# Output projection in scaled 16-bit halves, its weights resident from attention on, and the next layer's first weights made beside it

## Chip, cores, metric

One core of a Trainium2 chip runs the whole program. The metric is device time in microseconds (us), the median of several executions. The profile and the trace are of one execution.

## What is computed

Two layers of a token mixer, over 256 context tokens and 2048 latent tokens of width 1024. Each layer ends in one output projection and a gated residual. Cut from the reference:

```
for l in range(DEPTH):                      # DEPTH = 2, D = 1024
    shift, scale, gate = split(silu(c) @ w_mod[l] + b_mod[l], 3)
    h = rmsnorm(x, norm_g[l]) * (1 + scale) + shift
    f, g, (q, k, v, a) = branches(h @ w_in[l])        # Fourier, gated MLP, attention
    o = attention(q, k, v) * silu(a)                  # 8 heads, 2304 keys
    x = x + gate * (concat[f, g, o] @ w_out[l])       # w_out: 1024 x 1024
# the context rows y go the same way, in layer 0 alone
```

## The kernel before

A token tile is 128 rows; there are 18 (2 of context, 16 latent). A layer has three stages. The *blocks* normalise tiles and multiply them by five groups of input weights (group 0: keys, 416 columns; group 1: queries; groups 2 to 4: gates). *Attention* goes over heads and blocks of 512 queries. For each pair of key tiles TensorE makes the scores (`sc`), ScalarE takes two exponentials of each (a 16-bit `pp` and a 32-bit `pw`), GpSimd (one time in four VectorE) takes their difference, and TensorE multiplies both by the values (`pv`). VectorE reduces the row maxima (`mx`) of scores to come. Beside this runs a generator `background()`, advanced two steps a pair: the Fourier branch, then the gate vector (`modulate_turned(l, y, (2,), ..)`), and in layer 0 the small weights of layer 1 (`prepare`). The *output projection* follows: `mixed(t)` loads a tile of the concatenation, transposes it on TensorE and splits it into a high and a low part; `outward(l, y, t, n, ..)` makes half n of the output columns by `project`, 24 matmuls of 128x512 (8 chunks, three products: high x high, high x low, low x high), multiplies by the gate row `gr`, adds the residual and stores. In layer 0 `modulate_turned(l + 1, nxt, (0, 1), ..)` makes layer 1's shift and scale beside it: 32 loads into `mw`, two VectorE products with sums each.

All token products but the output projection use two 16-bit halves of each operand. The output projection uses two float32r parts: `weights` splits `w_out` (tags `wh`, `wl`, eleven buffers in pool W and five in pool X), and `mixed` takes one `h9` buffer a tile. Pool X opens only when attention's pool B has closed, so nothing that lives in it starts earlier.

Every operation is recorded first. A planner (`Plan.schedule`) with its own costs then gives each engine one fixed order, which may bring an operation forward past up to 1000 recorded ones where its buffers and operands allow it. All loads and stores are issued by SyncE, also in a fixed order. Since one helper emits everything, all instructions carry one line number (448).

Of the kernel before, what the change touches and what calls it, by code (L numbers as in the profile page):

```python
# [10 lines left out]
F32 = mybir.dt.float32  # L11
# [10 lines left out]
P = 128  # L22
D = 1024
# [38 lines left out]
XB = 6  # L62
# [487 lines left out]
def hybrid_kernel(ctx: ExitStack, tc: tile.TileContext, a: dict, out: bass.AP):  # L550
# [33 lines left out]
    def large():  # L584
        return mk(main, [P, T], F32R, "h9", 6)

# [3 lines left out]
    def k5():  # L590
        return mk(main, [P, NT * 65], F32, "k5")
# [325 lines left out]
    def operand():  # L917
        h = large()
        parts = h[:, :2 * D].rearrange("p (s k n) -> p s k n", s=2, k=KC)
        return parts[:, 0], parts[:, 1]  # L920

# [42 lines left out]

    def mixed(t):
# [12 lines left out]
        return hh, hl  # L978
# [26 lines left out]
    def weights(parts, wp, scale=None, extra=None):  # L1005
        n = sum(c for _, c in parts)
        wt = []
        for k in range(KC):
            wf = mk(wp, [P, NB], F32, "wf", WF)[:, :n]
            c0 = 0  # L1010
            for get, c in parts:
                get(k, wf[:, c0:c0 + c])
                c0 += c
            if extra and k >= WB - KC:
                wh, wl = (mk(extra, [P, NB], F32R, s, 2 * KC - WB) for s in ("wh", "wl"))
            else:
                wh, wl = (mk(wp, [P, NB], F32R, s, WB)[:, :n] for s in ("wh", "wl"))
            if scale is not None and k >= 4:
                v = scale[:, k - 4:k - 3]
                act.activation(out=wh, in_=wf, func=AF.Copy, scale=v)  # L1020
                dve.scalar_tensor_tensor(out=wl, in0=wf, scalar=v, in1=f(wh), op0=ALU.mult, op1=ALU.subtract)
            else:
                split(wh, wl, wf, pool if k % 2 else dve)
            wt.append((wh, wl))
        return wt

    def project(ht, wt, n):
        o = bank(tag="pj")
        hh, hl = ht
# [670 lines left out]
    for l in range(DEPTH):  # L1700
# [4 lines left out]
        def background():  # L1705
# [6 lines left out]
            load = lambda: mk(pools["W"], [P, NB], F32, "wh", WB)  # L1712
            for _ in modulate_turned(l, y, (2,), load):
# [8 lines left out]
        for b, blk in enumerate(blocks):  # L1722
# [7 lines left out]
            def done():  # L1730
# [3 lines left out]
        plan.close(pa)  # L1734
        pools["B"] = opened("B", "left")
        plan.close(wp)
# [4 lines left out]
        wp = pools["W"]  # L1741
        plan.close(pools["B"])
        px = opened("X", "left")
        tiles = list(range(0 if l < DEPTH - 1 else CT, NT))
        wt = [weights([(lambda k, dst, n=n: sp.dma_start(out=dst, in_=a["w_out"][l, k * P:(k + 1) * P, n * NB:(n + 1) * NB]), NB)], wp, y["vinv"], px if n else None)
              for n in range(2)]
        for t in tiles[:XB]:
            hts[t] = mixed(t)
        load = lambda: mk(px, [P, NB], F32, "mw", MW)
        ahead = iter(()) if l == DEPTH - 1 else modulate_turned(l + 1, nxt, (0, 1), load)  # L1750
        for t in tiles[:-XB]:
# [5 lines left out]
        for t in tiles[-XB:]:  # L1757
            outward(l, y, t, 0, hts[t], wt[0])
        for i, t in enumerate(tiles[-XB:]):
            outward(l, y, t, 1, hts[t], wt[1])  # L1760
            if l < DEPTH - 1 and i == 2:
                bounded(nxt)
# [3 lines left out]
        plan.close(px)  # L1766
        wt = {}
        plan.close(pools["C"])
        plan.close(wp)
        if l < DEPTH - 1:  # L1770
            pa_[0] = pa = opened("A", "left")
            wp = opened("W", "right")
            nxt["ic"] = [None] * 5
# [105 lines left out]
```

## Time and profile before

| | |
|---|---|
| median of 3 runs | 3146.82 us (3145.03 to 3150.45) |
| profiled execution, its own time | 3142.39 us |
| its span, first to last instruction | 3140.6 us |
| TensorE busy, granted clock (mean) | 2953.2 us (94%), 0.973 |
| VectorE, ScalarE, GpSimd busy | 2458.5, 1826.3, 1693.5 us |
| layer 0: blocks, attention, output projection | to about 650, 1430, 1677 us |
| layer 1: blocks, attention, output projection | to about 2200, 2932, 3140 us |

Busy TensorE time contains matmuls that overlap in the pipeline, so the time of a matmul in a stream is taken from start to start. A clock of 1.00 is 2.4 GHz; values below 1 are means over stretches at 2.4 and 1.2 GHz.

### The profile page before, as it was taken

What the parts mean: (1) busy time and instruction counts of PE and PEld (TensorE: products, weight loads), DVE (VectorE), ACT (ScalarE), POOL (GpSimd) and SP (SyncE); (2) the same over time, 40 slices, a digit from 0 to 9 for tenths busy, and PEclk for the clock granted to TensorE, in tenths of its full rate; (3) what the DMA queues carried; (4) which work ended last, traced back from release to release, by engine and by line L of the source; (5) the groups of instructions that cost most, each with busy time, mean ns of one, the idle gap of its engine ahead of it and who ended that gap; (6) DMA issues with size and microseconds to landing.
All of it is one profiled execution on the core that took longest, in us unless ns stands there. A gap on an engine that the chain in (4) does not pass through costs nothing.

```text
span 3140.6 us, 64404 instructions
## 1 busy us (share of the span) xinstructions
PE 2953.2 (94%) x23194; PEld 1724.2 (55%) x23194; DVE 2458.5 (78%) x6740; ACT 1826.3 (58%) x3904; POOL 1693.5 (54%) x1836
## 2 busy tenths in 40 slices
PE   6789999899999999998999999998999999999899
PEld 3445555445554555556785454553555555555687
DVE  7878788789999978765638888887899989887332
ACT  4553444167777788883006644531887887888400
POOL 3564444357667777772004744542876777777300
PEclk8899999999999999999999999998999999999999
DMA  7333344422324322205535343345023241230342
GB/s 271 69 73 58 84 94 87 102 88 67 86 61 131 81 72 61 57 23 177 175 118 192 62 86 86 87 96 142 24 64 79 71 125 49 61 75 20 111 134 81
DMA packets 487865, 289.08 MB, mean 92 GB/s; under 512 B 372316, under 2 KB 424180, under 8 KB 487544
## 3 DMA queue, kind: packets, MB, share of 16 engines
q1 hardware_dynamic: 487544, 284.96, 35.1%
q8 instruction: 182, 2.98, 0.4%
q14 instruction: 139, 1.14, 0.1%
HBM read 193.18 MB, written 91.66 MB: 91 GB/s over the span
## 4 chain that ended last, share of the span: by engine, by line
PE 59%; DVE 20%; DMA 8%; ACT 6%; POOL 3%; issue 2%; SPq 2%; DVEq 0%; ACTq 0%; POOLq 0%
PE pj L448 20%; PE sc L448 16%; PE pv L448 10%; PE mx L448 9%; DVE k L448 6%; DVE mx L448 4%; PE cb L448 3%; DMA k<-d 2%; ACT k L448 2%; SPq L448 2%; POOL k L448 2%; ACT pp L448 1%; DVE ns_t L448 1%; DMA mw<-in_w_modT_dram 1%; ACT pw L448 1%
## 5 line engine op out<-in xcount | busy, mean ns | idle before, releaser
L448 POOL TENSOR_TENSOR pp<-pw,pp 128x512 f16<-128x512 f32 (+1 forms) x876 | 1021.0, 1183 | 395.9 <-ACT pw L448 317.6
L448 PEld LDWEIGHTS <-h 128*128 128x128 f16 (+2 forms) x7008 | 581.8, 98 | 772.2 <-issue 410.2
L448 DVE TENSOR_REDUCE mx<-mx 128x1 f32<-128x512 f32 (+1 forms) x1296 | 770.9, 626 | 142.9 <-PE mx L448 136.9
L448 ACT ACTIVATE pp<-sc 128x512 f16<-128x512 f32 (+1 forms) x1168 | 717.5, 615 | 228.8 <-PE sc L448 215.5
L448 PE MATMUL sc<-h,h 128*128 128x512 f16 (+1 forms) x2336 | 602.8, 380 | 4.1 <-ACT pw L448 1.7
L448 ACT ACTIVATE pw<-sc 128x512 f32<-128x512 f32 (+1 forms) x876 | 543.7, 621 | 0.6 <-POOL pp L448 0.6
L448 PEld LDWEIGHTS <-pp 128*128 128x128 f16 x10432 | 467.3, 98 | 115.1 <-issue 32.5
L448 PE MATMUL pv<-k,pp 128*128 128x65 f16 (+2 forms) x10432 | 507.6, 203 | 7.6 <-DVE sm L448 7.0
L448 PE MATMUL mx<-h,h 96*128 96x512 f16 (+1 forms) x1296 | 410.4, 366 | 34.9 <-DVE mx L448 25.5
L448 PE MATMUL pj<-wh,h 128*128 128x512 f32 x1088 | 361.9, 405 | 7.3 <-DVE k L448 7.1
L448 PEld LDWEIGHTS <-hp 128*128 128x128 f16 x1920 | 187.8, 99 | 176.0 <-issue 14.3
L448 PE MATMUL pj<-w,h 128*128 128x512 f16 (+1 forms) x1296 | 272.2, 349 | 4.8 <-DVE tm L448 3.6
L448 PE MATMUL pj<-w,hp 128*128 128x512 f16 (+1 forms) x1152 | 241.4, 347 | 8.5 <-DVE tm L448 4.5
L448 POOL TENSOR_TENSOR h<-k,h 128x512 f16<-128x512 f32 (+1 forms) x72 | 80.8, 1138 | 299.6 <-ACT h L448 298.4
L448 PEld LDWEIGHTS pj<-wh,h 128*128 128x128 f32 x1088 | 208.6, 192 | 56.7 <-DVE k L448 11.1
L448 DVE TENSOR_TENSOR pp<-sc,pp 128x512 f16<-128x512 f32 (+1 forms) x292 | 197.8, 677 | 42.6 <-ACT sc L448 39.7
L448 PE MATMUL sc<-h 40*128 40x512 f16 (+1 forms) x1168 | 228.2, 387 | 0.0
L448 PE MATMUL pj<-wl,h 128*128 128x512 f32 x544 | 216.8, 399 | 0.0
L448 PE MATMUL pj<-h,h 128*128 128x416 f16 (+2 forms) x912 | 201.7, 363 | 6.5 <-ACT h L448 5.0
L448 DVE TENSOR_TENSOR pj<-pj,gr 128x512 f32<-128x512 f32 x68 | 47.3, 698 | 187.3 <-PE pj L448 187.3
L448 PE MATMUL pj<-h,hp 128*128 128x512 f16 (+1 forms) x768 | 174.4, 365 | 6.4 <-ACT hp L448 3.3
L448 ACT ACTIVATE sc<-sc 128x512 f32<-128x512 f32 (+1 forms) x292 | 178.8, 612 | 0.0
(270 smaller groups left out, 3936.7 us busy)
## 6 DMA issues: line engine op xcount, KB each, us to landing
d<-k SPq DMA_DIRECT2D x560, 48.0 KB
d<-k SPq DMA_DIRECT2D x166, 128.0 KB
d<-k SPq DMA_DIRECT2D x70, 256.0 KB
k<-d SPq DMA_DIRECT2D x132, 128.0 KB
k<-d SPq DMA_DIRECT2D x66, 256.0 KB
h<-d SPq DMA_DIRECT2D x24, 432.0 KB
d<-vt SPq DMA_DIRECT2D x144, 65.0 KB
k<-d SPq DMA_DIRECT2D x16, 585.0 KB
```

The costliest lines, as they stand in the source:

```text
L448: r = getattr(getattr(self.nc, eng), method)(*args, **kw)
```

## The change

`w_out` of the layer is loaded and split during attention by a new generator `output_weights`, into two float16 halves after scaling by a power of two (`power`, `halve` are the helpers that the other weights use). All 16 pieces stay in pool W (`wo`). `mixed` scales each row of its tile by a power of two from the row's sum of squares and splits into float16 halves, two tiles to a `h9` buffer; `outward` undoes both scalings in the gate multiplication. Tiles are prepared 4 ahead, not 6; `k5`, which holds a tile on its way in, has 3 buffers, not 2. In layer 0 `onward` makes shift and scale (into `mw` in pool W, 6 buffers of which 4 hold the condition vectors), then the weights of groups 0 and 2 of layer 1, in a new pool G. The order of the two halves changes: tile by tile to the end.

```diff
-TICKS = 2
+TICKS = 2, 1
+AHEAD_G = 2,
+OPACE = 3
-WB, WF = 11, 3
+WF = 3
-MW = 8
+MW = 6
-XB = 6
+XB = 4
     def k5():
-        return mk(main, [P, NT * 65], F32, "k5")
+        return mk(main, [P, NT * 65], F32, "k5", 3)
...
     def mixed(t):
         xt = k5()[:, :D]
...
-        hh, hl = operand()
+        ss = mk(small, [P, 1], F32, "ss")
+        act.activation(out=k2([P, D], BF16), in_=xt, func=AF.Square, accum_out=ss)
+        dve.tensor_scalar(out=ss, in0=ss, scalar1=2.0 ** -100, scalar2=2.0 ** 100, op0=ALU.max, op1=ALU.min)
+        pq = mk(small, [P, 2], F32, "mq", XB + 2)
...
+        dve.tensor_scalar(out=pq[:, 1:], in0=pq[:, 1:], scalar1=ow["pw"][:, 1:], scalar2=None, op0=ALU.mult)
+        act.activation(out=xt, in_=xt, func=AF.Copy, scale=pq[:, 0:1])
+        if t % 2 == 0:
+            mpair[0] = stacked()
...
         for half in range(2):
...
-            split(hh[:, 4 * half:4 * half + 4], hl[:, 4 * half:4 * half + 4], tp)
+            s = slice(4 * half, 4 * half + 4)
+            act.activation(out=hh[:, s], in_=tp, func=AF.Copy)
+            dve.tensor_tensor(out=hl[:, s], in0=tp, in1=hh[:, s], op=ALU.subtract)
...
+    def output_weights(l, y, wp):
+        w = mk(wp, [P, KC, 2, 2, NB], F16, "wo", 1)
+        am = mk(small, [P, 2 * KC + 1], F32, "wa", 1)
+        for k in range(KC):
+            for n in range(2):
+                sp.dma_start(out=whole(w[:, k, n]), in_=a["w_out"][l, k * P:(k + 1) * P, n * NB:(n + 1) * NB])
+                i = 2 * k + n
+                dve.tensor_reduce(out=am[:, i:i + 1], in_=whole(w[:, k, n]), axis=AX.X, op=ALU.max, apply_absolute_value=True)
+                yield
...
+        for k in range(KC):
+            for n in range(2):
+                halve(w[:, k, n], r[:, max(0, k - 3):max(0, k - 3) + 1], mk(wp, [P, NB], F32, "wf", WF))
+                yield
...
-        dve.tensor_tensor(out=o, in0=o, in1=y["gr"][1 if t < CT else 0][:, ns], op=ALU.mult)
+        dve.scalar_tensor_tensor(out=o, in0=o, scalar=ht[2], in1=y["gr"][1 if t < CT else 0][:, ns], op0=ALU.mult, op1=ALU.mult)
...
             gates(l, y, pools["C"])
+            for _ in output_weights(l, y, pools["W"]):
+                for _ in range(OPACE):
+                    yield
...
+        def onward():
+            for _ in modulate_turned(l + 1, nxt, (0, 1), lambda: mk(pools["W"], [P, NB], F32, "mw", MW)):
+                yield
+            bounded(nxt)
+            nxt["ic"] = [None] * 5
+            wt[0] = group(l + 1, nxt, 0, wp)
...
+            for g in AHEAD_G:
+                wt[g] = group(l + 1, nxt, g, wp)
...
+        for t in tiles:
             for n in range(2):
-                outward(l, y, t, n, hts[t], wt[n])
-                for _ in range(TICKS):
+                outward(l, y, t, n, hts[t], ow["w"][n])
+                for _ in range(TICKS[n]):
                     next(ahead, None)
-            hts[t + XB] = mixed(t + XB)
+            if t + XB < NT:
+                hts[t + XB] = mixed(t + XB)
```

VectorE at the end of layer 0's attention. The first piece is of before: its first products of `mw` for layer 1's shift stand behind the last attention work and among the splits of the projection (`h`, `wl`).

```order
L448 SCALAR_TENSOR_TENSOR wl_22749<-wf_19750,vinv_930,wh_22736 128x512
L448 SCALAR_TENSOR_TENSOR wl_22761<-wf_19817,vinv_930,wh_22742 128x512
L448 TENSOR_TENSOR h_4574_22708<-cx_22725,h_4574_22708 128x512
L448 TENSOR_TENSOR h_4588_22756<-cb_22744,h_4588_22756 128x512
L448 TENSOR_TENSOR h_4588_22756<-cx_22776,h_4588_22756 128x512
L448 SCALAR_TENSOR_TENSOR k_4594_22796,acc_22797<-mw_22734,mw_22715 128x512
L448 TENSOR_TENSOR pj_22657<-pj_22657,gr_3121_15553 128x512
L448 SCALAR_TENSOR_TENSOR k_4599_22812,acc_22797<-mw_22734,mw_22719 128x512
```

This piece is of the change, at the last two exponential differences (`pp`) of the same attention and the last `rc`, which ends it.

```order
L450 SCALAR_TENSOR_TENSOR k_4621_22749,acc_22397<-mw_22664,mw_19301 128x512
L450 SCALAR_TENSOR_TENSOR k_4626_22782,acc_22397<-mw_22664,mw_19317 128x512
L450 TENSOR_TENSOR pp_22784<-sc_22751,pp_22784 128x512
L450 SCALAR_TENSOR_TENSOR k_4633_22821,acc_22397<-mw_22723,mw_19298 128x512
L450 SCALAR_TENSOR_TENSOR k_4636_22828,acc_22397<-mw_22723,mw_19305 128x512
L450 SCALAR_TENSOR_TENSOR k_4639_22853,acc_22397<-mw_22819,mw_19301 128x512
L450 SCALAR_TENSOR_TENSOR k_4644_22894,acc_22397<-mw_22819,mw_19317 128x512
L450 TENSOR_TENSOR h_4596_22618<-cx_22861,h_4596_22618 128x512
L450 SCALAR_TENSOR_TENSOR k_4647_22910,acc_22397<-mw_22855,mw_19298 128x512
L450 SCALAR_TENSOR_TENSOR k_4650_22938,acc_22397<-mw_22855,mw_19305 128x512
L450 TENSOR_TENSOR h_4596_22618<-cx_22912,h_4596_22618 128x512
L450 RECIPROCAL rc_22958<-pv_22582 128x1
```

Of the 64 products, 48 now stand ahead of this last `rc` and 16 behind it; before, all 64 stood behind it.

TensorE at the border between layer 0 and layer 1. Before, the last product of layer 0 (`wh`) was followed by the two small transposes and products that find the scale of group 0 and group 1 (`am`, `pe`), and then by group 0's first matmul (`h,hp`, 416 columns).

```order
L448 MATMUL pj_24435<-wh_22830,h_4810_23991 128x512
L448 MATMUL cx_24523<-ident_163,k_4843_24319 128x128 x4
L448 MATMUL cb_24566<-ident_163,am_24321 1x128
L448 MATMUL cb_24594<-pe_24569,ones_157 128x2
L448 MATMUL cb_24605<-ident_163,am_24459 1x128
L448 MATMUL cb_24636<-pe_24613,ones_157 128x2
L448 LDWEIGHTS hp_24545
L448 MATMUL pj_24651<-h_4835_24272,hp_24545 128x416
```

In the change group 0's first matmul follows one normalisation transpose.

```order
L450 LDWEIGHTS h_4857_24352
L450 MATMUL pj_24778<-wo_13692,h_4857_24352 128x512
L450 MATMUL cx_24854<-ident_163,k_4876_24469 128x128 x4
L450 LDWEIGHTS h_4897_24657
L450 MATMUL pj_24860<-h_4756_23611,h_4897_24657 128x416
```

The scale of group 0 is found earlier, among the projection's tiles.

ScalarE near the end of layer 0's attention in the change: a Square and a scaling Copy of 128x1024, for tiles of the projection, stand among the exponentials. Two of each do so in either layer; before, none did.

```order
L450 ACTIVATE pw_21671<-sc_21618 128x512
L450 ACTIVATE pp_21682<-sc_21662 128x512
L450 ACTIVATE sc_21662<-sc_21662 128x512
L450 ACTIVATE sm_21773<-pv_21378 128x192
L450 ACTIVATE sm_21773<-pv_21378 128x64
L450 ACTIVATE k_3960_19557<-k_3960_19557,mq_21675 128x1024
L450 ACTIVATE pp_21796<-sc_21759 128x512
```

The Copy moved in front of the exponentials of the pair that follows.

## Rows read from the trace of the kernel before

**Rows 1.** Page, first part: busy us, share of the span, instructions.

```profile
PE 2953.2 (94%) x23194; PEld 1724.2 (55%) x23194; DVE 2458.5 (78%) x6740; ACT 1826.3 (58%) x3904; POOL 1693.5 (54%) x1836
```

**Rows 2.** Busy time by stretches of attention and output projection.

```profile
core 0: us, PE busy (x) PEld busy (x) DVE busy (x) ACT busy (x) POOL busy (x), PEclk, DMA share, GB/s
650.00:950.00 300.00, 292.89 (x3043) 167.59 (x3042) 282.78 (x622) 229.54 (x499) 205.36 (x191) 0.99 0.28 74
1250.00:1390.00 140.00, 135.34 (x1416) 74.53 (x1412) 111.28 (x241) 115.40 (x237) 103.55 (x100) 0.98 0.21 54
1390.00:1430.00 40.00, 39.13 (x483) 22.70 (x483) 10.93 (x24) 38.99 (x82) 35.50 (x34) 1.00 0.04 8
1430.00:1550.00 120.00, 102.26 (x481) 80.21 (x479) 79.63 (x208) 17.70 (x32) 3.52 (x4) 0.93 0.66 203
1550.00:1676.00 126.00, 126.00 (x580) 102.51 (x578) 52.38 (x114) 16.69 (x34) 4.83 (x8) 1.00 0.46 147
...
2890.00:2930.00 40.00, 39.13 (x470) 22.04 (x468) 12.65 (x26) 39.57 (x83) 34.47 (x33) 1.00 0.04 8
2930.00:2970.00 40.00, 32.83 (x210) 25.95 (x208) 15.66 (x25) 12.45 (x23) 5.31 (x6) 0.91 0.54 169
```

**Rows 3.** Chain that ended last, from 2900 us: start, duration, engine, what.

```profile
2934.15 5.35 DMA k<-d
...
3008.51 0.44 PE cx L448 x4
...
3081.67 52.65 PE pj L448 x228
```

**Rows 4.** TensorE in order of time, 1754 to 1761 us: start, us, operation, count.

```profile
1756.14 4.05 PE L448 MATMUL pj<-w,hp 128*128 128x512 f16 x18
1760.02 0.81 PE L448 MATMUL pj<-w,h 128*128 128x512 f16 x3
```

**Rows 5.** TensorE in order of time: the projections' ends, and layer 1's start.

```profile
1430.64 0.48 PE L448 MATMUL pj<-wh,h 128*128 128x512 f32 x1
...
1677.39 0.60 PE L448 MATMUL cx<-ident,k 128*128 128x128 f32 x4
...
1686.84 11.04 PE L448 MATMUL pj<-h,hp 128*128 128x416 f16 x48
...
1699.32 3.85 PE L448 MATMUL pj<-h,h 128*128 128x416 f16 x21 [0.27 <-ACT k L448]
1703.01 0.33 PE L448 MATMUL cx<-ident,ck 128*128 128x128 f32 x1
...
2932.45 0.48 PE L448 MATMUL pj<-wh,h 128*128 128x512 f32 x1
...
3135.31 0.39 PE L448 MATMUL pj<-wh,h 128*128 128x512 f32 x1
```

**Rows 6.** TensorE's waits, 1430 to 1690 us: total us, times, longest.

```profile
PE cx L448 <- DMA k<-d: 9.1, 6, 3.2
PE pj L448 <- DVE k L448: 7.1, 2, 3.7
```

**Rows 7.** Groups by shape: busy us, mean ns, idle before.

```profile
L448 DVE SCALAR_TENSOR_TENSOR k<-wh,wh 128x512 bf16<-128x512 f32 x64 | 58.6, 931 | 0.0
L448 DVE SCALAR_TENSOR_TENSOR k<-mw,mw 128x512 bf16<-128x512 f32 x64 | 40.9, 686 | 17.3 <-DMA mw<-in_w_modT_dram 14.4 <-DMA d<-k 1.5 <-DMA wf<-in_w_out_dram 1.3
L448 ACT ACTIVATE k<-k 128x1024 bf16<-128x1024 f32 x36 | 38.1, 1058 | 46.3 <-DMA k<-in_x_dram 17.2 <-DMA k<-d 15.8 <-DMA k<-in_ctx_dram 5.4
L448 POOL TENSOR_TENSOR w<-k,w 128x512 f16<-128x512 f32 x32 | 36.5, 1161 | 2.3 <-ACT w L448 2.3
L448 ACT ACTIVATE k<-w,wr 128x512 f32<-128x512 f32 x32 | 21.4, 712 | 2.1 <-DVE wr L448 1.5 <-POOL w L448 0.5
L448 DVE TENSOR_REDUCE am<-w 128x1 f32<-128x512 f32 x32 | 20.7, 671 | 0.4 <-DMA w<-in_w_g_dram 0.4
L448 ACT ACTIVATE w<-k 128x512 f16<-128x512 f32 x32 | 18.5, 618 | 0.0
```

More of the change, by code (lines that the diff above doesn't have):

```diff
@@ L914, in prepare @@
         yield
[L917 to L920, printed above, removed]
     hpair = [None]
@@ L963, in norm @@
         return hh, hl
+    mpair = [None]
     def mixed(t):
@@ L969, in mixed @@
         sp.dma_start(out=xt[:, 512:], in_=tokens(mo_d, t))
-        hh, hl = operand()
+        ss = mk(small, [P, 1], F32, "ss")
+        act.activation(out=k2([P, D], BF16), in_=xt, func=AF.Square, accum_out=ss)
+        dve.tensor_scalar(out=ss, in0=ss, scalar1=2.0 ** -100, scalar2=2.0 ** 100, op0=ALU.max, op1=ALU.min)
+        pq = mk(small, [P, 2], F32, "mq", XB + 2)
+        pi = pq.bitcast(I32)
+        dve.tensor_scalar(out=pi[:, 0:1], in0=ss.bitcast(I32), scalar1=-0.5, scalar2=1597463007.0 + float(TOP << 23),
+                          op0=ALU.mult, op1=ALU.add)
+        dve.tensor_scalar(out=pi[:, 0:1], in0=pi[:, 0:1], scalar1=EXPO, scalar2=None, op0=ALU.bitwise_and)
+        dve.tensor_scalar(out=pi[:, 1:], in0=pi[:, 0:1], scalar1=-1.0, scalar2=float(254 << 23), op0=ALU.mult, op1=ALU.add)
+        dve.tensor_scalar(out=pq[:, 1:], in0=pq[:, 1:], scalar1=ow["pw"][:, 1:], scalar2=None, op0=ALU.mult)
+        act.activation(out=xt, in_=xt, func=AF.Copy, scale=pq[:, 0:1])
+        if t % 2 == 0:
+            mpair[0] = stacked()
+        parts = mpair[0][:, t % 2, :2 * D].rearrange("p (s k n) -> p s k n", s=2, k=KC)
+        hh, hl = parts[:, 0], parts[:, 1]
         for half in range(2):
@@ L1003, in resident @@
         return [(v(k)[:, 0], v(k)[:, 1]) for k in range(KC)]
-    def weights(parts, wp, scale=None, extra=None):
-        n = sum(c for _, c in parts)
-        wt = []
+    ow = {}
+    def output_weights(l, y, wp):
+        w = mk(wp, [P, KC, 2, 2, NB], F16, "wo", 1)
+        am = mk(small, [P, 2 * KC + 1], F32, "wa", 1)
         for k in range(KC):
[L1009 to L1025, printed above, removed]
+            for n in range(2):
[3 more added lines that the diff above has]
+                yield
+        late = am[:, KC:2 * KC].rearrange("p (k n) -> p k n", n=2)
+        dve.tensor_tensor(out=late, in0=late, in1=y["vinv"].unsqueeze(2).to_broadcast([P, 4, 2]), op=ALU.mult)
+        dve.tensor_reduce(out=am[:, 2 * KC:], in_=am[:, :2 * KC], axis=AX.X, op=ALU.max)
+        pw = mk(lay, [P, 2], F32, "pwo")
+        power(am[:, 2 * KC:], pw)
+        r = mk(small, [P, 5], F32, "wq", 1)
+        dve.tensor_copy(r[:, 0:1], pw[:, 0:1])
+        dve.tensor_scalar(out=r[:, 1:], in0=y["vinv"], scalar1=pw[:, 0:1], scalar2=None, op0=ALU.mult)
+        yield
[3 more added lines that the diff above has]
+                yield
+        ow["pw"] = pw
+        ow["w"] = [[(w[:, k, n, 0], w[:, k, n, 1]) for k in range(KC)] for n in range(2)]
@@ L1027, in project @@
     def project(ht, wt, n):
         o = bank(tag="pj")
-        hh, hl = ht
+        hh, hl = ht[:2]
         for k in range(KC):
@@ L1711, in background @@
             pools["C"] = opened("C", "right")
-            load = lambda: mk(pools["W"], [P, NB], F32, "wh", WB)
-            for _ in modulate_turned(l, y, (2,), load):
+            for _ in modulate_turned(l, y, (2,), lambda: mk(pools["W"], [P, NB], F32, "mw", MW)):
                 for _ in range(PACE):
@@ L1734, in hybrid_kernel @@
         plan.close(pa)
+        if l:
+            plan.close(wp)
         pools["B"] = opened("B", "left")
-        plan.close(wp)
+        if not l:
+            plan.close(wp)
         banks("scores")
@@ L1740, in hybrid_kernel @@
         banks("project")
-        wp = pools["W"]
         plan.close(pools["B"])
-        px = opened("X", "left")
         tiles = list(range(0 if l < DEPTH - 1 else CT, NT))
-        wt = [weights([(lambda k, dst, n=n: sp.dma_start(out=dst, in_=a["w_out"][l, k * P:(k + 1) * P, n * NB:(n + 1) * NB]), NB)], wp, y["vinv"], px if n else None)
-              for n in range(2)]
         for t in tiles[:XB]:
             hts[t] = mixed(t)
-        load = lambda: mk(px, [P, NB], F32, "mw", MW)
-        ahead = iter(()) if l == DEPTH - 1 else modulate_turned(l + 1, nxt, (0, 1), load)
-        for t in tiles[:-XB]:
+        wt = {}
+        def onward():
+            for _ in modulate_turned(l + 1, nxt, (0, 1), lambda: mk(pools["W"], [P, NB], F32, "mw", MW)):
+                yield
+            bounded(nxt)
+            nxt["ic"] = [None] * 5
+            wt[0] = group(l + 1, nxt, 0, wp)
+            yield
+            yield
+            for g in AHEAD_G:
+                wt[g] = group(l + 1, nxt, g, wp)
+                yield
+                yield
+        ahead = iter(())
+        if l < DEPTH - 1:
+            wp = opened("G", "left")
+            ahead = onward()
+        for t in tiles:
             for n in range(2):
-                outward(l, y, t, n, hts[t], wt[n])
-                for _ in range(TICKS):
+                outward(l, y, t, n, hts[t], ow["w"][n])
+                for _ in range(TICKS[n]):
                     next(ahead, None)
-            hts[t + XB] = mixed(t + XB)
[L1757 to L1762, printed above, removed]
+            if t + XB < NT:
+                hts[t + XB] = mixed(t + XB)
+            if l < DEPTH - 1 and t == NT - 3:
+                run(ahead)
                 for u in BLOCKS[l + 1][0]:
@@ L1765, in hybrid_kernel @@
                         hts[u] = norm(l + 1, nxt, u)
-        plan.close(px)
-        wt = {}
         plan.close(pools["C"])
-        plan.close(wp)
+        plan.close(pools["W"])
         if l < DEPTH - 1:
             pa_[0] = pa = opened("A", "left")
-            wp = opened("W", "right")
-            nxt["ic"] = [None] * 5
             for t in BLOCKS[l + 1][0]:
```

4 lines of the change are left out of this document (1 added, 3 removed).

## Prediction

> **What bounds the kernel now.** The page comes first: TensorE is busy for 94% of the span, the others far less [rows 1], so what counts is what TensorE does longer than it must and where it waits. The stretches say where. In attention TensorE is full, with VectorE nearly full beside it early on (282.78 of 300 us), and in the last 40 us with ScalarE full too (38.99 and 39.57) while VectorE has little to do [rows 2]. The output projection has two faces. Its first 120 us in layer 0 show TensorE busy for 102.26 us at a clock of 0.93 with the DMA engines at 0.66; after that it is busy without a gap at 1.00. Layer 1's first 40 us look like layer 0's start [rows 2]. TensorE's waits name the cause: the tile that comes in (`k<-d`) 9.1 us, VectorE 7.1 us in two stalls [rows 6]; in layer 1 the chain passes through such a load of 5.35 us and ends in one run of projection matmuls [rows 3]. At the border of the layers TensorE stands from 1677.39 to 1686.84 but for a transpose, and then starts slowly [rows 5].
>
> **The matmuls.** There are 68 half tiles of 24, so 1632, before and after. In the chain's last run 228 float32r ones take 52.65 us, 0.2309 us each [rows 3]. The 16-bit form with the same shapes runs already in the blocks: 18 take 1760.02 - 1756.14 = 3.88 us, 0.2156 each, with their weight loads under them [rows 4]. Both are at full clock. 1632 x 0.0153 = **25.0 us less**. Both durations have rows of their own, so I give this term no range.
>
> **The waits at the projection's start.** Layer 0 goes from 1430.64 to 1677.39, 246.75 us [rows 5]. The work in it is 864 x 0.2309 = 199.5, 41 groups of four transposes at 0.44 = 18.0 [rows 3], and one group of `pv` products of 0.7 us: 218.2. So 28.5 us are lost; 16.2 are the two waits in the rows, and 120 x 0.07 = 8.4 the clock below 1 [rows 2, 6]. Layer 1 takes from 2932.45 to 3135.70 [rows 5], 203.25 us, for 177.3 + 31 x 0.44 + 0.7 = 191.6; 11.6 are lost. The change acts on this in three ways. `k5` has three buffers, so two tiles wait normalised when attention ends (the order shows two Squares and two Copies ahead of it) where one did; that is 96 matmuls, 21 us of work, over a load of 5.35 us and a chain of Square, scaling, transposes and split of about 5 us (1.058 twice, 0.44 twice, 0.618, a few short ones on VectorE). The 4 MB of `w_out` are gone from the crowded start, and of the 64 products of `mw` only 16 stay behind attention, 11 us of VectorE at 0.686 [rows 7] instead of 44. Against it stands the longer chain a tile, 2.1 us of ScalarE, which has 16.69 us of work in 126 [rows 2], and five short VectorE operations, which is at 52.38 in 126. Nothing else is queued behind them that TensorE needs within a tile's 10 us. I take that 8 us of the 28.5 and 5 of the 11.6 remain, since the last head's output must still go out and come back. **20.5 and 6.5 us less**; bounds 0 (another wait of equal size) to all 40.1.
>
> **The border.** From 1677.39 to 1686.84 only one transpose group runs: 9.0 us lost. The 48 matmuls that follow take 10.88 us until the next, where 416 columns cost (1703.01 - 1699.32) / 21 = 0.1757, so 8.43 [rows 5]: 2.45 more, at a clock of 0.79 [rows 2]. In the change group 0's first matmul follows the projection directly, and the 16 reductions for group 0 and group 2 (at most 0.671 each [rows 7]) are done before. What is late next are the normalised tiles 2 and 3: their buffers are in pool A, which still opens only when the projection is done, and the 48 matmuls of tiles 4 and 5 cover 8.4 us. I leave 3 of 11.5 us: **8.5 less**; bounds 0 and 11.5.
>
> **Attention pays.** *ScalarE.* Halving is two operations a piece, 0.712 + 0.618 [rows 7], so 21.3 us a layer; the eleven splits that ran there before were one each, 6.8 us at 0.618. Net 14.5 us. In the planned order the 32 stand within some 28 pairs in layer 0 and 24 in layer 1, at about 2.5 us a pair 70 and 59 us, where ScalarE is at about 115.4/140 = 82% [rows 2]. That asks for 8 and 11 us more than there are. TensorE can take up maxima that are due later, so I charge 3 and 5 (bounds 0 and 29 together). The two Squares and Copies a layer fall into the stretch where ScalarE is full [rows 2]: 4 x 1.058 and half a split, 4.8 us a layer; I charge 4 each (bounds 0 and 9.6), **8 and 8 us more**. *VectorE.* 48 products move under attention. There, products of the same form cost 0.931, against 0.686 in the projection, where GpSimd rests [rows 7]: 44.7 us. With 16 reductions of 0.671, and without the eight of the eleven splits that VectorE shared in (taken at the same price), the net is 50.0 us in layer 0 and 5.4 in layer 1. They fall mostly between 1250 and 1430, where VectorE has 122 us of work in 180; with them it is at 93%, as in 650 to 950, where TensorE lost 7 us of 300 [rows 2]. I charge **7 us** for both layers (bounds 0 and 55). GpSimd's 16 halvings a layer at 1.161 [rows 7] are 18.6 us at about 74% [rows 2]; the differences `pp` queue behind them for one operation at a time, which four `sc` banks and ten `pp` buffers hold. I charge nothing for that.
>
> Here a rule speaks against the change. The 0.931 beside 0.686 [rows 7] shows that such a product waits for GpSimd now and then. The Trainium skill, SBUF — State Buffer, section "Who interferes with whom", says that a VectorE instruction with two SBUF inputs contends with a GpSimd one that reads SBUF and that whoever starts first holds the port for its whole instruction, while reductions never contend; the trace agrees. If each moved product met a whole GpSimd operation, then by an estimate from that rule 48 x 1.161 = 55.7 us of waiting would stand in place of the 48 x 0.245 = 11.8 in the measured price, and the sum would be 37.5 - 43.9 if all of it reached TensorE; the mean of 0.931 says that one product in five does.
>
> **What is hidden or equal.** The DMA bytes are the same: `w_out` and `mw` are loaded once, earlier. SyncE issues the `w_out` loads in two clusters during attention, ahead of nothing that is due within them. The two free `mw` buffers make each load wait for a product; under attention the DMA share is 0.04 to 0.28, so a load comes quickly, and behind the `mw` products on VectorE stand one `pp` difference in four and the maxima, which have a lead. The third `k5` buffer also lets layer 0's first tiles come one earlier; I count nothing for it, with 5 us either way.
>
> **Sum.** 25.0 + 27.0 + 8.5 - 8 - 8 - 7 = 37.5 us less. The profiled execution's own time of 3142.39 becomes 3104.9; the median of the runs shown is 4.4 above that execution and becomes 3109.3. I give **3107**, from the middle of the two starts, 3144.6, as for the rivals; with the costs of attention at half or at one and a half it is 3095 to 3119.
>
> **Rivals.**
> *Attention costs nothing* (0.20): TensorE is the bound there and has its maxima to fill in. All 60.5 us stay: 3084. For it speaks that ScalarE and VectorE have slack as means over the stage; against it the full ScalarE of the last 40 us.
> *The start stays as slow* (0.18): the longer chain a tile and SyncE's fixed order take what the third buffer gives. Then 25.0 + 8.5 - 23 = 10.5 us less: 3134. For it speaks that the last head's output must pass through DRAM in any case; against it, that before there was one buffer to wait on.
> *VectorE becomes attention's bound* (0.06): every one of the added 55.4 us, and the 16 us of ScalarE, falls on the path. 60.5 - 55.4 - 16 = -10.9, so 3156. It ends slower once more than 44.5 of the 55.4 us of VectorE reach TensorE, since 60.5 - 16 = 44.5. Against it: after 1390 VectorE is at 10.93 of 40 [rows 2].
> *The move doesn't happen* (0.06): TensorE's order is as printed, but the products left behind wait for their loads as now (the longest stretch of such idling sums to 14.4 us [rows 7]), so that group 0's scale is late again. The border's 8.5 and 14.4 of the start are lost: 37.5 - 22.9 = 14.6 less, 3130.
> The forecast has the remaining 0.50.
>
> The range of 3080 to 3135 takes in the first, the second and the fourth and leaves out the third and the tails. A measurement of this kernel tells 0.2%, 6 us, from no change. The forecast, the first and most of the second and fourth are faster by more: 0.90; 0.04 within it; 0.06 slower.
>
> **What would show it.** 128x512 `pj<-wo` matmuls at 0.216 from start to start. Few `cx <- DMA k<-d` waits after attention, and no stall on VectorE in the projection of layer 0; a projection of about 213 us there and of 185 in layer 1. Group 0's first matmul within 3 us of the last `wo` one, at a clock near 1. In attention a stage longer by some 10 us in either layer, with `PE sc <- ACT` or `mx <- DVE mx` waits where the halvings and the products stand. I am wrong if attention grows by more than 30 us, if the first tiles still wait 5 us each, or if the clock falls within the projection though no wait shows.

## The result and the profile after

The changed kernel takes 3100.98 us (median of 4 runs, 3098.44 to 3103.97) against 3145.93 before, a ratio of 0.9859 with a 95% interval of 0.9839 to 0.9879; the forecast was 3107, in a range of 3080 to 3135. The profiled execution took 3103.97 us itself.

The page's first part (busy us, share, instructions) answers to [rows 1]: TensorE is busy 30 us less and still bounds the kernel; VectorE has 50 us more to do, ScalarE 94.

```profile
PE 2922.8 (94%) x23200; PEld 1577.3 (51%) x23200; DVE 2508.6 (81%) x6938; ACT 1920.3 (62%) x4038; POOL 1734.6 (56%) x1860
```

Busy time by stretches of layer 0's attention and projection, with the columns of [rows 2]. VectorE is now nearly full until attention ends, where before it had little to do in the last 40 us. The projection still loses time in its first 30 us, at a clock of 0.89.

```profile
1240.00:1390.00 150.00, 146.71 (x1553) 80.19 (x1551) 134.97 (x310) 128.00 (x263) 119.44 (x108) 0.98 0.25 69
1390.00:1428.00 38.00, 35.07 (x415) 20.01 (x415) 33.19 (x65) 34.57 (x72) 35.83 (x29) 1.00 0.18 57
1428.00:1460.00 32.00, 26.39 (x153) 14.23 (x154) 22.11 (x67) 13.36 (x22) 4.86 (x5) 0.89 0.65 196
1460.00:1550.00 90.00, 85.75 (x419) 42.34 (x418) 44.99 (x131) 27.88 (x42) 0.00 (x0) 0.98 0.54 165
1550.00:1651.00 101.00, 100.36 (x499) 49.69 (x497) 59.19 (x152) 37.78 (x74) 17.40 (x20) 1.00 0.60 195
```

TensorE in order of time (start, us, operation, count, idle before it and its releaser). It answers to [rows 4, 5]: nine matmuls of the new form go from 1627.67 to 1629.61, 0.2156 us each. Two waits of over 4 us are left near the start, and group 0's first matmul follows the projection's last transposes without a gap.

```profile
1428.41 0.81 PE L450 MATMUL pj<-wo,h 128*128 128x512 f16 x3
...
1429.76 2.11 PE L450 MATMUL pj<-wo,h 128*128 128x512 f16 x9
...
1433.56 5.99 PE L450 MATMUL pj<-wo,h 128*128 128x512 f16 x27
1444.19 1.11 PE L450 MATMUL cb<-ident,k 128*128 128x128 f32 x4 [4.64 <-ACT k L450]
...
1445.95 5.27 PE L450 MATMUL pj<-wo,h 128*128 128x512 f16 x15
...
1451.93 3.40 PE L450 MATMUL pj<-wo,h 128*128 128x512 f16 x15
...
1479.81 11.56 PE L450 MATMUL pj<-wo,h 128*128 128x512 f16 x45 [4.25 <-DVE k L450]
...
1627.67 2.11 PE L450 MATMUL pj<-wo,h 128*128 128x512 f16 x9
1629.61 0.60 PE L450 MATMUL cx<-ident,k 128*128 128x128 f32 x4
...
1650.50 0.60 PE L450 MATMUL cx<-ident,k 128*128 128x128 f32 x4
1650.94 1.75 PE L450 MATMUL pj<-h,h 128*128 128x416 f16 x9
```

TensorE's waits from 1428 to 1660 us (total, times, longest) answer to [rows 6]. The loads `k<-d` are gone as a releaser. The scaling Copy behind them (`ACT k`) has taken their place with 5.1 us where they had 9.1, and VectorE's evictions of finished sums (`DVE k`) are at 4.9 us where they were at 7.1.

```profile
PE cb L450 <- ACT k L450: 5.1, 2, 4.6
PE pj L450 <- DVE k L450: 4.9, 2, 4.3
```

**Stage by stage.** The stages of a trace lie between these points: the first maxima of attention (`mx<-h,h`), the first `pj<-wo` (or `pj<-wh`), the end of the last of these (there the projection ends and the border begins), the start of the 96th matmul by `h` weights behind it (end of the border), the first scores of layer 1, and its own first and last `pj<-wo`. All in us. The second row of the changed kernel is a second trace of it, from an experiment below; where the two differ, by up to 3.3 us, is what a single trace cannot tell. The last column is the median of all runs; the kernel before, run again beside each group of experiments, took 3144.48 to 3147.81.

| kernel | layer 0: blocks | attention | projection | border, 96 matmuls | layer 1: other blocks | attention | projection | median |
|---|---|---|---|---|---|---|---|---|
| before | 618.8 | 811.8 | 246.9 | 30.7 | 486.2 | 738.0 | 203.3 | 3145.93 |
| after | 609.2 | 819.2 | 222.3 | 23.0 | 489.7 | 744.2 | 189.6 | 3100.98 |
| after_again | 607.4 | 815.9 | 221.9 | 22.6 | 488.8 | 744.6 | 191.5 | 3100.08 |
| k5_two | 619.7 | 816.7 | 226.3 | 20.3 | 476.2 | 744.7 | 194.5 | 3107.01 |
| before_k5_three | 607.9 | 813.0 | 247.0 | 30.5 | 495.6 | 736.5 | 202.8 | 3136.04 |
| mw_behind | 604.7 | 807.6 | 241.5 | 22.2 | 488.0 | 744.7 | 190.7 | 3106.10 |
| mw_paced | 605.6 | 834.4 | 223.3 | 21.7 | 488.6 | 747.9 | 191.1 | 3117.88 |
| no_halving | 606.5 | 814.5 | 222.2 | 23.2 | 488.8 | 747.4 | 189.9 | 3101.82 |
| no_scaling | 604.9 | 819.7 | 222.7 | 22.1 | 491.8 | 741.0 | 186.0 | 3090.07 |
| chain_on_pool | 606.4 | 821.2 | 220.6 | 22.9 | 491.9 | 746.0 | 187.4 | 3101.17 |
| no_early_groups | 607.3 | 819.4 | 215.6 | 32.3 | 476.3 | 746.9 | 190.5 | 3093.61 |
| group0_only | 607.6 | 818.9 | 217.4 | 20.4 | 511.2 | 744.6 | 188.9 | 3116.31 |
| group0_pool | 607.5 | 820.4 | 213.5 | 20.5 | 510.5 | 746.9 | 189.5 | 3114.76 |
| chain_pool_late | 606.6 | 819.1 | 214.5 | 32.9 | 476.3 | 747.9 | 188.7 | 3093.36 |

Of the 38.5 us by which the first two traces differ at the last projection matmul, the projections and the border give 46.0, layer 0's blocks, where only the buffers of `k5` were changed, 9.6; the two attentions take back 13.6 and the rest of layer 1's blocks 3.5. With the second trace of the changed kernel it is 43.0 us: 44.9 and 11.4, less 10.7 and 2.6. The medians differ by 45.0.

### The profile page after: what moved, and what is told of

It reads as the page before. It is cut to its first block, busy times and chain, and to the rows that moved or that the text cites. A ratio compares the mean times of both kernels' runs of the same rounds, so it can differ in the third digit from the quotient of the medians.

```text
span 3101.9 us, 64730 instructions
## 1 busy us (share of the span) xinstructions
PE 2922.8 (94%) x23200; PEld 1577.3 (51%) x23200; DVE 2508.6 (81%) x6938; ACT 1920.3 (62%) x4038; POOL 1734.6 (56%) x1860
## 5 line engine op out<-in xcount | busy, mean ns | idle before, releaser
L450 POOL TENSOR_TENSOR pp<-pw,pp 128x512 f16<-128x512 f32 (+1 forms) x876 | 1035.0, 1199 | 366.1 <-ACT pw L450 276.7
L450 PEld LDWEIGHTS <-h 128*128 128x128 f16 (+2 forms) x8640 | 741.0, 98 | 975.4 <-issue 435.9
L450 ACT ACTIVATE pp<-sc 128x512 f16<-128x512 f32 (+1 forms) x1168 | 735.1, 632 | 230.6 <-PE sc L450 220.3
L450 ACT ACTIVATE pw<-sc 128x512 f32<-128x512 f32 (+1 forms) x876 | 557.3, 639 | 0.8 <-POOL pp L450 0.7
L450 PE MATMUL pj<-wo,h 128*128 128x512 f16 x1632 | 368.1, 383 | 6.5 <-DVE k L450 6.5
L450 ACT ACTIVATE k<-k 128x768 f16<-128x768 f32 (+1 forms) x140 | 133.1, 951 | 235.0 <-DMA k<-d 114.5
L450 PE MATMUL pj<-h,hp 128*128 128x416 f16 (+1 forms) x768 | 175.6, 363 | 6.7 <-ACT k L450 4.8
L450 ACT ACTIVATE k<-pj,pw 128x256 f32<-128x256 f32 (+4 forms) x208 | 93.1, 455 | 139.4 <-PE pj L450 126.8
L450 DVE STREAM_TRANSPOSE k<-k 128x384 f16<-128x384 f16 x280 | 144.5, 553 | 18.2 <-ACT k L450 13.4
```

The lines of the kernel that those rows point to most:

```text
L450: r = getattr(getattr(self.nc, eng), method)(*args, **kw)
```

## Experiments

**The third buffer.** Two kernels take the `k5` buffer away from the changed kernel, and give it to the kernel before.

```diff
-        return mk(main, [P, NT * 65], F32, "k5", 3)
+        return mk(main, [P, NT * 65], F32, "k5")
```

> The changed kernel with two `k5` buffers again where it has three. Its layer 0 reaches the first maxima of attention 9.1 us earlier than before, though no line of the blocks was changed. Theory A: the third buffer does this, because the blocks load their tiles into `k5` too; it also gives the projection one more normalised tile. Then the first maxima come 8 to 10 us later than in the changed kernel, the two projections grow by 3 to 8 us together, and the time is 3112 to 3119 us. Theory B: the 9.1 us come from how loads and engines happened to fall in that execution; then the blocks stay within 3 us and the time is 3101 to 3108.

> The kernel before with three `k5` buffers and nothing else. Theory A (the third buffer by itself is worth 9 us in the blocks of layer 0, whatever the projection does): 3134 to 3139 us, with the first maxima 8 to 10 us earlier than before; the projection's first waits for `k<-d` get shorter by at most 5 us. Theory B (it is worth nothing without the rest of the change): 3143 to 3149.

Alone it makes the kernel before 11 us faster (0.9966, interval 0.9955 to 0.9977), and layer 0's blocks end near 608 us with it and near 619 without, in both kernels: theory A on the mechanism. `fetch` puts the blocks' tiles into `k5`, so with three buffers a third tile is under way at the program's start: the first load `k<-in_x` goes out at 29.08 us where it went at 44.17, the next at 44.37 where it went at 55.70. In the kernel before, ScalarE's Square waits for this later tile, and TensorE behind it; with three buffers neither wait is in the trace. At the first `mx<-uk` of the blocks the two kernels with two buffers are at 83.3 and 83.4 us and the other twelve traces at 74.9 to 77.5, so most of the gain is made by then.

```profile
55.70 0.36 SPq L448 DMA_DIRECT2D k<-in_x_dram  x1
...
62.23 1.06 ACT L448 ACTIVATE k<-k 128x1024 bf16<-128x1024 f32 x1 [3.49 <-DMA k<-in_x_dram]
...
67.21 0.88 PE L448 MATMUL pj<-h,hp 128*128 128x416 f16 x2 [3.27 <-ACT hp L448]
```

Without it the changed kernel's projections are longer by 4.0 and 4.9 us (4.4 and 3.0 against the second trace), as theory A said; those of the kernel before are the same with and without. But the time of the changed kernel rose by 6 us, which is in theory B's range, not by 11 or more, since layer 1's other blocks were 13 us shorter: the planner's order changes there too. In the kernel before they are 9 us longer with the third buffer. Why was not taken apart.

**The products under attention.** One kernel keeps all 64 products of `mw` behind attention: their loads go into a pool X that opens there, and the gate vector's, which used the same buffers in attention, into a pool N of its own. The other puts all 64 into the background of attention at a step of two.

```diff
-            for _ in modulate_turned(l + 1, nxt, (0, 1), lambda: mk(pools["W"], [P, NB], F32, "mw", MW)):
+            for _ in modulate_turned(l + 1, nxt, (0, 1), lambda: mk(pools["X"], [P, NB], F32, "mv", MW)):
...
```

> The changed kernel with the tiles of `w_modT` for layer 1 in a pool that opens only when attention is done, so that none of the 64 products can move under layer 0's attention. In the changed kernel SyncE issues the loads of `mw` and of the projection's tiles in one order, and from 1412.8 to 1429.0 us it stands at `mw` loads that wait for products on VectorE; the third tile's load goes out behind them. Theory A: this keeps the third tile late, and the products cost attention some 7 us. Then the wait of 4.6 us for the third tile falls below 1.5 us, attention of layer 0 is 5 to 8 us shorter, and the time is 3090 to 3098 us. Theory B: the tile is late because the last head's output passes DRAM and the DMA engines are crowded; then the wait stays at 4 to 5 us, the 64 loads add to the crowd, the projection is 5 to 10 us longer, and the time is 3101 to 3110.

> The changed kernel with all 64 products for layer 1's shift and scale in attention's background, spread at a step of two, where 48 run there in a cluster at its end and 16 in the projection. With all of them behind attention the projection was 19.2 us longer and attention 11.6 us shorter. Theory A: VectorE's queue in the projection is what the products harm; with the last 16 gone it is 3 to 8 us shorter (214 to 219 us), attention grows by 2 to 5, and the time is 3095 to 3101 us. Theory B: SyncE's loads for more products hold up the tiles' loads at attention's end; then the first wait of the projection grows above 4.6 us and the time is 3102 to 3110.

With the 48 products behind it, attention is 8 to 12 us shorter, but the projection 19 us longer: theory A is right only in that attention pays for the products, and the time is in theory B's range. TensorE waited in the projection for VectorE and for the tiles. In the last 43 us of attention and the first 22 of the projection SyncE stood 35.6 us for products (`DVE k`) in the changed kernel and not at all in this one, and the tiles came late all the same; so they can be late without SyncE standing at `mw` loads. The 64 loads of the products now crowd the same start, so this kernel does not say what else makes them late.

```profile
PE pj L450 <- DVE k L450: 16.3, 6, 4.7
PE cb L450 <- ACT k L450: 9.8, 3, 3.5
```

With all 64 under attention it grows by another 15 to 19 us, and the projection gains nothing (223.3); its first wait for a tile is 3.9 us: both theories fall. The stretch below, of that kernel, shows VectorE at 93% and TensorE at 135.75 of 150 us with a clock of 0.93; with none of them there (second fence, the kernel with the products behind) TensorE is full.

```profile
1240.00:1390.00 150.00, 135.75 (x1310) 70.56 (x1309) 140.14 (x347) 106.64 (x221) 102.57 (x93) 0.93 0.29 79
```

```profile
1240.00:1390.00 150.00, 149.89 (x1612) 82.04 (x1610) 111.16 (x256) 133.38 (x275) 116.54 (x113) 1.00 0.15 36
```

**The added ScalarE work.** One kernel leaves out the halving, one the Square, the short VectorE operations and the scaling Copy of each tile.

```diff
-                halve(w[:, k, n], r[:, max(0, k - 3):max(0, k - 3) + 1], mk(wp, [P, NB], F32, "wf", WF))
+                pool.memset(w[:, k, n], 0.5)
```

```diff
-        act.activation(out=k2([P, D], BF16), in_=xt, func=AF.Square, accum_out=ss)
...
-        act.activation(out=xt, in_=xt, func=AF.Copy, scale=pq[:, 0:1])
```

> Leaves out the halving of `w_out` (two ScalarE and one GpSimd operation a piece); GpSimd writes a constant into the piece instead, so the matmuls keep their shapes and multiply a constant. Theory A: the halvings cost attention what was charged, 3 us in layer 0 and 5 in layer 1; then attention goes from 819 to 812 to 817 us and from 778 to 771 to 775, and the time is 3090 to 3096 us. Theory B: the halvings fit into ScalarE's slack and cost nothing; then attention stays within 2 us in each layer and the time is 3099 to 3103.

> Leaves out each tile's Square, its five VectorE operations and its scaling Copy; the split takes a constant factor instead. Theory A: this longer chain is what keeps the first tiles of a projection late, 5.1 and 4.2 us of waits for ScalarE, and the evictions behind it; then the projections go from 222.3 to 212 to 216 us and from 189.6 to 183 to 186, attention's last stretch gets 1 to 4 us shorter in each layer, and the time is 3082 to 3091 us. Theory B: the tiles are late because their loads are; then TensorE waits as long, for `DMA k<-d` by name as before the change, and the time is 3096 to 3102.

Without the halving the time is the same, 3101.82 us; attention is 1 to 5 us shorter in layer 0 and 3 longer in layer 1, about what two traces of one kernel differ by: theory B. (The 778 us that the expectation names for layer 1's attention is 744 by the table.) Without the scaling the time falls by 11 us, into theory A's range: 3.2 to 3.6 of it stand in layer 1's attention and 3.6 to 5.5 in its projection, 2.5 to 4.3 in layer 0's blocks, which the edit doesn't touch. But layer 0's projection stays at 222.7, and so does its attention: there theory A is wrong. With the chain gone TensorE waits for a load again, 2.2 us where it waited 5.1 for the scaling, and longer than in the changed kernel for the evictions, 7.0 us for 4.9:

```profile
PE pj L450 <- DVE k L450: 7.0, 2, 5.7
PE cx L450 <- DMA k<-d: 2.2, 1, 2.2
```

**VectorE's queue.** VectorE runs its operations in order, and the clamp of a tile's sum of squares (`ss`) stands in front of evictions that TensorE needs. In the changed kernel's projection of layer 0 it idles 61.2 us for Squares, 2.33 of them just before the eviction that ends TensorE's wait at 1479.81:

```profile
1477.69 0.15 DVE L450 TENSOR_SCALAR ss<-ss 128x1 f32<-128x1 f32 x1 [2.33 <-ACT k L450]
...
1478.29 0.74 DVE L450 SCALAR_TENSOR_TENSOR pj<-pj,mq,gr 128x512 f32<-128x512 f32 x1
1479.06 0.69 DVE L450 TENSOR_TENSOR k<-pj,k 128x512 f32<-128x512 f32 x1
```

```profile
DVE ss L450 <- ACT k L450: 61.2, 15, 7.8
DVE k L450 <- DMA mw<-in_w_modT_dram: 5.5, 3, 3.0
```

The next kernel moves the five short operations to GpSimd, which has 0.00 us of work from 1460 to 1550 (with rounding in place of the integer mask).

```diff
-        dve.tensor_scalar(out=ss, in0=ss, scalar1=2.0 ** -100, scalar2=2.0 ** 100, op0=ALU.max, op1=ALU.min)
+        pool.tensor_scalar(out=ss, in0=ss, scalar1=2.0 ** -100, scalar2=2.0 ** 100, op0=ALU.max, op1=ALU.min)
...
```

> The changed kernel with the five short operations that make a tile's power of two (clamp, two integer steps, inverse, product) on GpSimd in place of VectorE. In layer 0's projection VectorE idles 61.2 us in 15 waits for a tile's Square, and the operations that free TensorE's banks stand in its queue behind the clamp; TensorE waits 4.9 us for those. Theory A: the order of VectorE's queue is what stops TensorE; then TensorE's waits for `DVE k` fall below 1 us, the projection of layer 0 goes from 222.3 to 214 to 218 us, layer 1's from 189.6 to 186 to 189, and the time is 3091 to 3098 us. Theory B: the tile itself is late; then the banks come free sooner, but TensorE waits as long for the tile, the projections stay within 3 us, and the time is 3099 to 3104.

The idling for Squares falls to 6.4 us, but that for `mw` loads doubles, and TensorE waits as long for the evictions, 5.3 us for 4.9. The projection is 1 to 2 us shorter, the time the same: theory B, by another wait than it named.

```profile
DVE k L450 <- DMA mw<-in_w_modT_dram: 10.2, 4, 3.6
DVE ss L450 <- ACT k L450: 6.4, 3, 2.8
```

**The early groups.** The first kernel leaves shift and scale beside the projection but makes groups 0 and 2 only behind it, the second makes group 0 alone early.

```diff
-            wt[0] = group(l + 1, nxt, 0, wp)
...
-            wp = opened("G", "left")
...
+            wp = opened("W", "right")
```

```diff
-AHEAD_G = 2,
+AHEAD_G = ()
```

> The changed kernel with shift and scale of layer 1 made beside the projection, but the weights of its groups 0 and 2 only behind it, in a pool W opened as before. Theory A: the border of the layers is what the early groups give, 7 us by the traces; TensorE stands 7 to 10 us there again, and the time is 3106 to 3112 us. Theory B: what they cost beside the projection (their loads at 90% busy DMA engines, their reductions ahead of the evictions on VectorE, the stall of 4.25 us at 1479.8 us) is as much as they give; then the projection of layer 0 is 5 to 8 us shorter, and the time is 3099 to 3103.

> The changed kernel with only group 0's weights made beside the projection, and group 2's behind it as before. In the order of SyncE eight loads of group 2's weights stand among the loads of the first six tiles, where the DMA engines are 70 to 90% busy; here they stand at its end. Theory A: these loads are what keeps the start of layer 0's projection slow; then it takes 214 to 218 us instead of 222.3, the border stays below 1 us, and the time is 3090 to 3097 us. Theory B: the crowd is made by `mw` and the last head's output, not by them; then the projection takes 220 to 224 us and the time is 3098 to 3104.

Without early groups the border costs 9.3 us more, and the projection 6.7 less. The kernel came out below both theories, at 3093.61 us, because layer 1's other blocks were 13 us shorter. With group 0 alone the border stays closed and the projection is 4.7 us shorter (theory A), but the time is 15 us worse: group 2's weights are late next, and layer 1's other blocks take 22 us more. TensorE of that kernel waits for `ck`, which ScalarE makes from values of VectorE, and for `pe` of VectorE, while VectorE, busy for 19.14 of 20 us, works on these values and on the reductions of group 2; the clock falls.

```profile
1671.09 0.47 PE L450 MATMUL cx<-ident,ck 128*128 128x128 f32 x1 [5.12 <-ACT ck L450]
...
1681.62 0.58 PE L450 MATMUL cb<-pe,ones 1*128 1x2 f32 x2 [3.08 <-DVE pe L450]
```

```profile
1664.00:1684.00 20.00, 9.58 (x31) 3.84 (x29) 19.14 (x88) 10.74 (x28) 7.01 (x16) 0.65 0.18 44
```

**Both together, and the changed kernel again.** Two kernels join the edits: group 0 alone early with the short operations on GpSimd, and no early group with them. They ran on one chip with the changed kernel itself.

> The changed kernel once more, to tell what belongs to its order and what to one execution. Theory A: the order sets the stages; the blocks of layer 0 end at 604 to 610 us, the projections take 220 to 224 and 188 to 191 us, the last stretch of layer 1's blocks has its waits of 2 and 4 us for `DVE tm` again and the clock falls behind them, and the time is 3098 to 3104 us. Theory B: the 12 us by which the kernel without early groups was shorter at the end of layer 1's blocks were chance; then that stretch is 8 to 12 us shorter here too, and the time is 3090 to 3096.

> As the kernel with group 0 alone made early, and the short operations of a tile's power of two on GpSimd. Theory A: with fewer loads at the start what is left of TensorE's waits for `DVE k` is the order of VectorE's queue; then layer 0's projection takes 211 to 215 us and the time is 2 to 5 us less than with group 0 alone. Theory B: VectorE then waits for `mw` loads instead of for Squares, as it did with this edit alone; the projection and the time stay within 2 us of group 0 alone.

> Neither group made early, and the short operations of a tile's power of two on GpSimd. Theory A (the early groups cost the projection about what the border gains, and the end of layer 1's blocks follows from the order): the border is 9 to 11 us, layer 0's projection 212 to 216 us, layer 1's blocks 495 to 500 us from the border's end to attention's first scores, and the time 3089 to 3095 us. Theory B (the shorter blocks of layer 1 came from one execution): blocks of 505 to 512 us, and 3099 to 3106.

The changed kernel repeats: 3100.08 us (0.9850, interval 0.9829 to 0.9871), and the same stages. With group 0 alone the projection goes from 217.4 to 213.5 us, as theory A said, but the time falls by 1.6 us only, as theory B said. The kernel with neither group early takes 3093.36 us (0.9833, interval 0.9812 to 0.9854), and its layer 1 blocks are short again: theory A. Its five runs and the four of the kernel without early groups lie at 3087.9 to 3097.1, the eight of the changed kernel at 3096.7 to 3104.0. So two versions are some 7 us faster than the changed kernel.

Where these 13 us of layer 1's blocks are shows in the stretch ahead of its attention. The changed kernel first:

```profile
2095.00:2100.00 5.00, 2.44 (x20) 1.36 (x19) 4.28 (x19) 0.00 (x0) 1.32 (x2) 1.00 0.21 81
...
2105.00:2110.00 5.00, 1.02 (x3) 0.43 (x4) 4.33 (x12) 2.23 (x4) 3.44 (x5) 0.85 0.11 15
2110.00:2115.00 5.00, 5.00 (x21) 2.02 (x19) 4.59 (x25) 0.92 (x2) 1.37 (x2) 0.81 0.54 95
...
2125.00:2130.00 5.00, 1.57 (x10) 0.59 (x8) 0.00 (x0) 0.00 (x0) 0.14 (x1) 0.90 0.85 243
2130.00:2135.00 5.00, 5.00 (x19) 2.32 (x18) 2.12 (x4) 0.00 (x0) 0.00 (x0) 0.50 0.82 254
```

and the kernel without early groups, where the longest wait there is 2.0 us:

```profile
2085.00:2125.00 40.00, 36.10 (x194) 17.26 (x193) 32.35 (x125) 9.44 (x18) 18.28 (x22) 1.00 0.53 116
```

In the changed kernel TensorE waits 2.45 and 4.03 us for VectorE (`tm`) and 3.42 us for a load of attention, and the clock falls behind the last two. That the orders differ is shown; which edit of the planner's input makes it so (pool G open in layer 1, its closing ahead of B, or the order alone) was not tried.

## Why the prediction was right, and where its steps were off

**The matmuls: right.** 0.2156 us each, as forecast: 25.0 us.

**The projections' starts: mis-sized.** I left 8 and 5 us of loss. The work in the changed kernel is 864 x 0.2156 + 18.0 + 0.7 = 205.0 and 768 x 0.2156 + 13.6 + 0.7 = 179.9 us, so 17.3 and 9.7 are lost, and 13.1 us were gained where I put 27.0. Two steps failed.

One is "that is 96 matmuls, 21 us of work". Two tiles did stand ready, but TensorE's fixed order has only 3 + 9 + 27 = 39 of their matmuls ahead of the transposes of the third tile (rows above; the same in the second trace), and there it waited 4.64 us (3.77). I had counted what was ready, not what the order puts first. In every version of the change that scales, one of layer 0's first tiles cost such a wait, 2.5 to 4.6 us; in that without the scaling it became one of 2.2 us for a load. An order with more of the 96 in front was not tried.

The other is "nothing else is queued behind them that TensorE needs within a tile's 10 us". The making of group 2's weights is: in the six traces that have it beside the projection (with three `k5` buffers and not all products behind attention) the stage takes 220.6 to 223.3 us, in the four without it 213.5 to 217.4. Whether its loads, which stand among those of the first six tiles, or its reductions on VectorE do this is not shown, for the edit takes away both. The order of VectorE's queue is a small part at most: moving the short operations took 1.7, 3.9 and 1.1 us off the projection in three pairs of single traces, and at most 1.6 off the time. I had also set down the loads as equal in bytes; they were (289.1 MB in both kernels), but not in place: group 2's came into the crowded start. The 213.5 us of the kernel with both edits are the 213 that I forecast for the change itself.

**The border: right.** 7.7 us for 8.5; from 1651 to 1674 the clock is 1.00, where the kernel before has the 0.79 that I named:

```profile
1676.00:1700.00 24.00, 16.56 (x77) 8.91 (x77) 18.79 (x57) 18.82 (x41) 17.25 (x28) 0.79 0.94 322
```

The price in the projection was missing: for both groups 6.7 us.

**Attention: too dear by 9 us, and only in part for the reasons given.** I charged 23 us; the traces show 7.4 (4.1 in the second) and 6.2 (6.6). The 8 us for the halving were nothing that can be told. The 8 for Squares and Copies were 3 to 4 in layer 1, hardly more than two traces of one kernel differ by, and none in layer 0. The products cost what I said or somewhat more, 8 to 12 us for 7; that is more than layer 0's attention grew by. The waits that I named for attention did grow, `mx <- DVE mx` by some 3 us in either layer, and those for `sm`, the last step of a `pv` sum, 5.6 us before, are gone from layer 0. The first two rows are of layer 0 before, the third of layer 0 in the changed kernel, the last two of layer 1 before and after:

```profile
PE mx L448 <- DVE mx L448: 15.2, 22, 3.7
PE pv L448 <- DVE sm L448: 5.6, 3, 4.5
...
PE mx L450 <- DVE mx L450: 18.4, 25, 4.7
...
PE mx L448 <- DVE mx L448: 6.1, 11, 3.2
...
PE mx L450 <- DVE mx L450: 9.0, 14, 2.8
```

The products' mean in the changed kernel's attention was 1.067 us, not 0.931 [rows 7], and 0.685 behind attention with GpSimd at rest:

```profile
L450 DVE SCALAR_TENSOR_TENSOR k<-mw,mw 128x512 bf16<-128x512 f32 x46 | 48.8, 1067 | 2.7 <-DMA mw<-in_w_modT_dram 2.7
```

```profile
L450 DVE SCALAR_TENSOR_TENSOR k<-mv,mv 128x512 bf16<-128x512 f32 x64 | 41.5, 685 | 9.8 <-DMA mv<-in_w_modT_dram 9.4
```

The means alone, 0.382 us more against 1.157 of a GpSimd halving, would say that one product in three met a whole operation of GpSimd, and [rows 7] one in five. Taken one by one the records say otherwise: of the 45 that begin in this stretch 15 took 0.66 to 0.70 us and 30 took 0.75 to 1.67; before, 22 of the 64 under attention took more than 0.75, the longest 1.68; and the 64 with GpSimd at rest all lie between 0.67 and 0.70. So two in three were delayed, each by part of an operation (at most 0.98 us), and one in three not at all. By the rule of the Trainium skill, SBUF — State Buffer, section "Who interferes with whom", that I set beside it, such a pair excludes each other; these two rows agree that products take longer where GpSimd works, and the records show that not all do. No run here separates the port from other causes.

**Not priced.** The third buffer, which I set to nothing "with 5 us either way", is worth 10 to 11 us in layer 0's blocks: I looked at `k5` in `mixed` and not at its other users. In layer 1's blocks, which I did not price either, 3.5 us were lost; the third buffer or the new order can be the cause, and the runs above show both to move these blocks by 9 to 22 us.

So 25.0 + 13.1 + 7.7 + 9.6 - 13.6 - 3.5 = 38.3 us stands beside my 37.5: the total was met by luck, by errors that cancel: 14 us too much at the starts against 9 too dear in attention and 6 not priced.

**The rivals.** That attention costs nothing was half right, that the start stays as slow was half right too. VectorE did not become the bound with 48 products; with 64 in another order it nearly did, at 17 us more in the time, so the cost is not in proportion to their number. The move happened.

## What to carry to other kernels

Before pricing a larger buffer count, list every stage that uses that tag: here it was worth more in the blocks than where it was meant to work. Work brought forward is paid where it lands, so look in the queues of the place for what its loads and reductions stand in front of, and for what is late next if only part of it moves (15 us here). Where the order is fixed, count the work that it puts ahead of a wait (39 matmuls), not the work that is ready (96). And a sum that comes out right says little on its terms; the stages of two traces do.

## What the hardware showed beyond that

A wait costs TensorE more than itself. Behind the 4.64 us up to 1444.19, the granted clock is at 0.50 in the next 4 us, that is 1.2 GHz, and fifteen matmuls take 5.27 us where fifteen behind them take 3.40 (rows above), at 1.00 from 1452 on: 1.9 us more. Behind 4.25 us of idling at 1479.8 it is at 0.57:

```profile
1440.00:1444.00 4.00, 0.00 (x0) 0.00 (x0) 0.97 (x7) 2.05 (x3) 0.17 (x1) 0.86 0.71 215
1444.00:1448.00 4.00, 3.81 (x13) 2.44 (x14) 2.40 (x7) 3.24 (x6) 0.00 (x0) 0.50 0.34 111
...
1480.00:1484.00 4.00, 4.00 (x12) 1.51 (x11) 2.79 (x8) 1.15 (x1) 0.00 (x0) 0.57 0.77 181
```

The length of a wait does not tell by itself whether the clock falls. The one of 2.0 us ahead of layer 1's attention in the kernel without early groups left it at 1.00 (row above). In the kernel without the scaling a wait of 2.22 us was followed by a clock of 0.66 from 1436 to 1440 us, and twelve matmuls took 4.44 us; in the kernel with the products behind attention one of 3.15 us (third row) was followed by 1.00 from 1431 to 1435. In both the clock stood at 1.00 before the wait (1432 to 1436, 1427 to 1431); what makes the difference these runs do not show.

```profile
1436.58 0.63 PE L450 MATMUL cx<-ident,k 128*128 128x128 f32 x4 [2.22 <-DMA k<-d]
1437.04 4.44 PE L450 MATMUL pj<-wo,h 128*128 128x512 f16 x12
...
1431.63 0.66 PE L450 MATMUL cb<-ident,k 128*128 128x128 f32 x4 [3.15 <-ACT k L450]
```
